# Forgetting, selected-block and dilated attention heads taken two at a time, one in each half of the partitions

## The chip, the cores and the metric

The kernel runs on one core of a Trainium2 chip. The metric is device time in microseconds (us) of one execution; less is better. The median of three runs before the change is 2567.84 us (2560.59 to 2719.17).

## The reference

Two transformer blocks run on one sequence of 256 tokens with 2048 features, all in fp32. The change lies in the first block's mixer: `proj = u @ w_in` is split into the inputs of four kinds of attention, whose outputs are joined and go through `w_out`.

```python
# forgetting ("fox"): 7 heads of 64
s = q @ k * scale + cq[..., None] - cum[:, :, None, :]; p = softmax(causal(s)); o = p @ v
# selected-block ("nsa"): 8 heads of 64 in 2 groups; the keys and values of a group are shared
o = g0 * o_cmp + g1 * o_selected + g2 * o_window        # three softmaxes with three sets of keys
# dilated: 9 heads of 64 in 3 groups of 3; heads i, 3+i, 6+i share a softmax over their log-sums
w = softmax(stack(lses)); o = concat(o_g * w_g)
# differential: 4 heads with two score maps of 64 each and a value of 128
o = (softmax(s0) - lam * softmax(s1)) @ v
h = h + g1 * (concat(o_fox, o_nsa, o_dil, o_diff) @ w_out)
```

The rest (norms, the modulation vectors `c_act @ ada_w`, the gated feed-forward layer, and the second block with a band attention, a recurrent mix and a memory attention) is the same before and after. With 256 tokens, 4 blocks of 64 and 16 blocks to select, every causal block is selected, so each head's scores are plain causal scores.

## The kernel before

Features lie on the partitions. A weight matrix is read in pieces of 512 KB by the SP queue (`piece`, L291), cast by ACT into a rounded part `Wh` (L293), and the rest `Wl` is left by DVE (L294); there are three buffers of each. TensorE then runs eight matmuls of 512 columns with `Wh` (both parts of the activations side by side) and eight of 256 columns with `Wl`, all recorded at L189 as `pd<-s,Wh` and `pd<-s,Wl` (`unit_b`). `unit_a` has the activations stationary instead (`pd<-Wh,s`, `pd<-Wl,s`). Call these the dense stream.

Side work is written as Python generators. After each piece `step` advances every active one to its next `yield`, and `later(n, ...)` starts one n pieces on (`AT`: fox heads 4 pieces apart, nsa heads 5, dilated triples 4). `trickle` adds pieces of the modulation vectors: a 512 KB load (L196) and a weighted sum on DVE (L432), 0.5 to 1.0 of them a piece. A scheduler then fixes each engine's order; every engine follows its own, and waits on semaphores.

A head's side work is: `table` (L196) loads its 128x256 mask and slope table into one of three buffers; `scores` makes the scores of both query blocks in one bank of PSUM with two matmuls (64 rows contracted, 128x256 and 128x128), and a fox head adds two that contract 7 rows for its decay; DVE adds the table and takes the maximum (L590), ACT exponentiates with a sum (L594), and weighs (`weigh`, L600); `pt` transposes the map in three matmuls (L193, `ps<-con,e`) and ACT copies it out (L609); `pv` multiplies by the values (`ps<-pt,s`, 64 output partitions); `put` writes the half-height result as a rounded part (ACT, L627) and a rest (DVE, L628). An nsa head does scores, weighing and transposes twice, and sums three value products (the first, of the compressed branch, shows as `ps<-s 128*64`) in one bank. PSUM has four banks for side work and four for the dense stream.

fp32 matmuls show as two records each, so a 64-row score set (two matmuls) is four records, a fox set eight.

Heads h and h+1 of fox lie in opposite halves of the partitions, as do nsa heads j and j+4. The 24 results of 64 rows fill twelve tiles in the order of the heads.

Of the kernel before, what the change touches and what calls it, by code (L numbers as in the profile page):

```python
# [129 lines left out]
NARROW = {"start"}  # L130

# [16 lines left out]
class Build:  # L148
# [424 lines left out]
    def scores(self, q, k, tab, fox=None):  # L573


        nc = self.nc
        p = self.ps()
        last = fox is None
        self.mm(p[:, 0:256], q[:, 128:256], k, True, last)
        if not last:  # L580
            self.mm(p[:, 0:256], fox[0], fox[1], False, True)
        self.mm(p[:, 256:384], q[:, 0:128], k[:, 0:128], True, last)
        if not last:
            self.mm(p[:, 256:384], fox[0], fox[1][:, 0:128], False, True)
        e = self.tmp((128, 384), tag="e")
        m = self.tiny(2)
        nm = self.tiny(2)
        sm = self.tiny(2)
        for a, (lo, hi, t0) in enumerate(((0, 256, 0), (256, 384, 128))):
            nc.vector.tensor_tensor_reduce(e[:, lo:hi], p[:, lo:hi], tab[:, t0:256], scale=1.0, scalar=-3e38,  # L590
                                           op0=OP.add, op1=OP.max, accum_out=m[:, a:a + 1])
        nc.vector.tensor_scalar(nm, m, -1.0, None, op0=OP.mult)  # L592
        for a, (lo, hi) in enumerate(((0, 256), (256, 384))):
            nc.scalar.activation(e[:, lo:hi], e[:, lo:hi], AF.Exp, bias=nm[:, a:a + 1],  # L594
                                 accum_out=sm[:, a:a + 1])
        return e, m, sm
# [38 lines left out]
    def fox_head(self, h):  # L635
        q, k = self.hq[h], self.hk[h]
        tab = self.table(0)
        yield from self.wait(lambda: self.ncum is not None)
        e, m, sm = self.scores(q, k, tab, (self.sel7[h], self.ncum))
        self.weigh(e, self.recip(sm))  # L640
        yield
        t = self.pt(e)
        yield
        hf = (h % 2) * 64
        p = self.ps()[hf:hf + 64, :256]
        self.pv(p, self.fv[0][:, 64 * h:64 * h + 64], self.fv[1][:, 64 * h:64 * h + 64], t)
        self.put(h, p)

    def fox_cum(self):
# [28 lines left out]
        yield  # L678
        p = self.ps()
        self.mm(p[:7, 0:128], a[:, 0:7], self.C["trif"])  # L680
        self.mm(p[:7, 128:256], a[:, 0:7], self.ones, True, False)
        self.mm(p[:7, 128:256], a[:, 7:14], self.C["trif"], False, True)
        t = self.slot()
        v.tensor_copy(t[:7, :256], p[:7, :256])
        self.ncum = t[:7, :256]
# [100 lines left out]
    def nsa_head(self, h):  # L786
        nc = self.nc
        g = h // 4
        hf = 64 * g
        q = self.nq[h % 4][hf:hf + 64]  # L790
        n = 7 + h
        tab = self.table(1 + h)
        es = []
        yield
        for br, k in ((1, self.nks), (2, self.nkw)):
            e, m, sm = self.scores(q, k[hf:hf + 64], tab)
            f = self.recip(sm)
            for a in range(2):
                nc.vector.tensor_tensor(f[:, a:a + 1], f[:, a:a + 1], self.gate[:, 1 - a, h, br:br + 1], op=OP.mult)
            self.weigh(e, f)  # L800
            es.append(e)
            yield
        ts = [self.pt(e) for e in es]
        yield from self.wait(lambda: self.pct is not None)
        yield
        of = (n % 2) * 64
        p = self.ps()[of:of + 64, :256]
        self.mm(p, self.vcb[:, h, :], self.pct, True, False)
        for b in range(2):
            c = b * 128 + g * 64  # L810
            self.pv(p, self.nv[0][:, c:c + 64], self.nv[1][:, c:c + 64], ts[b], False, b == 1)
        self.put(n, p)

    def dil_triple(self, i):
        nc, v = self.nc, self.nc.vector
        M = self.tiny(6)
        Z = self.tiny(6)
        es = []
        for g in range(3):
            h = 3 * g + i  # L820
            tab = self.table(9 + h)
            yield
            e, m, sm = self.scores(self.dq[h], self.dk[h], tab)
            v.tensor_copy(M[:, 2 * g:2 * g + 2], m)
            v.tensor_copy(Z[:, 2 * g:2 * g + 2], sm)
            es.append(e)
        mx = self.tiny(2)
        v.tensor_tensor(mx, M[:, 0:2], M[:, 2:4], op=OP.max)
        v.tensor_tensor(mx, mx, M[:, 4:6], op=OP.max)
        M3 = M.rearrange("p (g a) -> p g a", g=3)  # L830
        v.tensor_tensor(M3, M3, mx[:, None, :].to_broadcast([128, 3, 2]), op=OP.subtract)
        nc.scalar.activation(M, M, AF.Exp)
        v.tensor_tensor(Z, Z, M, op=OP.mult)
        z = self.tiny(2)
        v.tensor_tensor(z, Z[:, 0:2], Z[:, 2:4], op=OP.add)
        v.tensor_tensor(z, z, Z[:, 4:6], op=OP.add)
        r = self.recip(z)
        v.tensor_tensor(M3, M3, r[:, None, :].to_broadcast([128, 3, 2]), op=OP.mult)
        for g in range(3):
            self.weigh(es[g], M[:, 2 * g:2 * g + 2])  # L840
        yield
        for g in range(3):
            h = 3 * g + i
            n = 15 + h
            t = self.pt(es[g])
            yield
            of = (n % 2) * 64
            p = self.ps()[of:of + 64, :256]
            vv = self.dv[0 if h < 5 else 1]
            c = 64 * (h if h < 5 else h - 5)  # L850
            self.pv(p, vv[0][:, c:c + 64], vv[1][:, c:c + 64], t)
            self.put(n, p)
# [16 lines left out]
    def diff_head(self, h):  # L869
# [4 lines left out]
        for m in range(2):  # L874
            e, _, sm = self.scores(self.fq[h][64 * m:64 * m + 64], self.fk[h][64 * m:64 * m + 64], tab)
            es.append(e)
            fs.append(self.recip(sm))
# [9 lines left out]
        self.pv(p, self.fvv[0][:, 128 * h:128 * h + 128], self.fvv[1][:, 128 * h:128 * h + 128], t)  # L887
# [16 lines left out]
    def mixer(self):  # L904
        self.narrow = "mixer" in NARROW
        I, X = self.I, self.X
        w = "w_in"
        self.consts(1)
        sel = [self.slot(), self.slot()]
        self.load(sel[0][:7, :512], I["const2"][:7, :512])  # L910
        self.load(sel[1][:7, :384], I["const2"][:7, 512:])
# [876 lines left out]
```

## Time and profile before

| what | before |
|---|---|
| runs, median of 3 | 2567.84 us |
| profiled execution, own time | 2565.86 us |
| its span | 2563.7 us |
| PE busy | 2478.7 us (97%) |
| DVE busy | 1793.0 us (70%) |
| ACT busy | 1294.2 us (50%) |
| granted TensorE clock, mean | 0.981 |

The profile is of one execution. Its own time is the span from the first to the last instruction and 2.2 us around it. Busy times are unions of an engine's instructions, so overlapping matmuls count once. In a timeline, rows of like instructions are merged: the first number is the start of the first, the second the time to the end of the last, and `x4` their number. The start of a row to the start of the next row is what the engine spent on it.

### The profile page before, as it was taken

To read this page: it belongs to the slowest core of one execution; us is meant where nothing else is said; L and a number is where in the kernel's file an instruction comes from. 1 tells how busy PE (TensorE), PEld (TensorE's weight loads), DVE (VectorE), ACT (ScalarE), POOL (GpSimd) and SP (SyncE) were. 2 spreads that over 40 slices of the span, in tenths; PEclk is the share of its full clock that TensorE was granted. 3 is DMA by queue.
4 is the path that set the end of the run, shared out by engine and by line. 5 is a ranking of instruction groups with operands and counts; after the bars stand their busy time and mean duration, and the time that the engine had idled before them with its cause. 6 is when DMAs were issued, how large, how long until landed. Compare 5 with 4: busy or idle time off the path is not lost.

```text
span 2563.7 us, 39188 instructions
## 1 busy us (share of the span) xinstructions
PE 2478.7 (97%) x14820; PEld 2124.7 (83%) x14820; DVE 1793.0 (70%) x3371; ACT 1294.2 (50%) x2177; POOL 55.7 (2%) x102
## 2 busy tenths in 40 slices
PE   6889999998799999999999999999999999999999
PEld 5678888777688888888888878888888888888888
DVE  8987777689767765555566887659885666666664
ACT  5354455665544444444455554546553554444443
POOL 0000000000000000000000002000110000000000
PEclk8999999999899999999999999999999999999999
DMA  9998777678578866666655656324554366666675
GB/s 326 340 341 286 247 240 267 203 232 270 181 247 277 277 212 190 192 189 188 188 183 183 204 177 181 108 79 149 166 157 124 97 193 189 189 188 190 189 229 166
DMA packets 161500, 527.57 MB, mean 206 GB/s; under 512 B 22912, under 2 KB 33175, under 8 KB 161184
## 3 DMA queue, kind: packets, MB, share of 16 engines
q1 hardware_dynamic: 157296, 516.41, 62.7%
q0 software_dynamic: 4016, 8.66, 1.1%
q8 instruction: 116, 1.90, 0.3%
q14 instruction: 72, 0.59, 0.1%
HBM read 516.60 MB, written 9.45 MB: 205 GB/s over the span
## 4 chain that ended last, share of the span: by engine, by line
PE 71%; issue 12%; DVE 8%; DMA 5%; ACT 2%; POOL 1%; SPq 0%; DVEq 0%; ACTq 0%; POOLq 0%
PE pd L189 64%; PE ps L189 6%; DVE Wl L294 3%; DVE b L432 2%; DMA b<-in_ada_w_dram 2%; DMA W<-in_w_mem_kv_dram 1%; DMA W<-in_w_out_dram 1%; ACT Wh L293 1%; PE ps L193 1%; DMA W<-in_w_in_dram 1%; POOL q L1283 0%; DMA tq<-qd 0%; DVE dt L224 0%; DVE e L590 0%; DVE q L1061 0%
## 5 line engine op out<-in xcount | busy, mean ns | idle before, releaser
L189 PE MATMUL pd<-s,Wh 128*128 128x512 f32 (+1 forms) x5824 | 1450.2, 391 | 37.5 <-ACT Wh L293 19.1
L294 DVE TENSOR_TENSOR Wl<-W,Wh 128x1024 fp32r<-128x1024 f32 x770 | 927.8, 1207 | 546.7 <-ACT Wh L293 519.8
L293 ACT CAST Wh<-W 128x1024 fp32r<-128x1024 f32 x770 | 796.8, 1036 | 957.6 <-PE pd L189 596.7
L189 PEld LDWEIGHTS pd<-s,Wh 128*128 128x128 f32 x5824 | 1032.5, 192 | 225.9 <-ACT Wh L293 24.1
L189 PEld LDWEIGHTS pd<-s,Wl 128*128 128x128 f32 x5584 | 769.4, 192 | 65.8 <-DVE Wl L294 11.2
L189 PE MATMUL pd<-s,Wl 128*128 128x256 f32 x5584 | 795.8, 285 | 6.8 <-DVE Wl L294 6.7
L432 DVE SCALAR_TENSOR_TENSOR b<-b,tq 128x1024 f32<-128x1024 f32 x192 | 233.0, 1221 | 51.0 <-DMA b<-in_ada_w_dram 50.7
L189 PE MATMUL pd<-Wh,s 128*128 128x512 f32 (+4 forms) x576 | 164.0, 363 | 4.3 <-ACT Wh L293 4.3
L189 PEld LDWEIGHTS pd<-Wh,s 128*128 128x128 f32 x576 | 103.8, 189 | 21.7 <-ACT Wh L293 6.2
L224 DVE TENSOR_TENSOR dt<-pd,dt 128x256 f32<-128x256 f32 x289 | 110.7, 418 | 11.0 <-ACT dt L223 10.3
L189 PE MATMUL pd<-Wl,s 128*128 128x512 f32 (+4 forms) x288 | 105.2, 365 | 5.5 <-DVE Wl L294 5.5
L223 ACT COPY dt<-pd 128x256 f32<-128x256 f32 x289 | 94.6, 370 | 22.8 <-PE pd L189 20.9
L189 PE MATMUL ps<-s 128*128 128x256 f32 (+7 forms) x356 | 88.7, 384 | 4.4 <-DVE tab L1555 2.3
L189 PEld LDWEIGHTS ps<-s 64*128 64x128 f32 (+4 forms) x356 | 57.4, 192 | 27.8 <-issue 13.7
L189 PEld LDWEIGHTS pd<-Wl,s 128*128 128x128 f32 x288 | 54.7, 190 | 16.1 <-DVE Wl L294 8.9
L594 ACT ACTIVATE e<-e,y 128x256 f32<-128x256 f32 x80 | 35.7, 449 | 30.3 <-DVE y L592 30.3
L189 PE MATMUL ps<-q,con 128*128 128x256 f32 x132 | 40.0, 410 | 8.4 <-ACT q L1033 2.9
L209 DVE TENSOR_TENSOR s<-q,s 128x256 fp32r<-128x256 f32 x104 | 40.0, 421 | 5.0 <-ACT s L208 4.7
L208 ACT CAST s<-q 128x256 fp32r<-128x256 f32 x104 | 37.9, 405 | 8.2 <-DVE q L1084 4.9
L189 PE MATMUL ps<-pt,s 128*64 128x128 f32 (+3 forms) x176 | 37.6, 343 | 1.7 <-ACT pt L609 1.7
L600 ACT ACTIVATE e<-e,y 128x256 f32<-128x256 f32 x88 | 35.0, 450 | 6.5 <-DVE y L632 3.8
L590 DVE CUSTOM_DVE_ANT_0 e<-ps,tab 128x256 f32<-128x256 f32 x80 | 26.1, 352 | 16.4 <-PE ps L189 16.1
(291 smaller groups left out, 1400.0 us busy)
## 6 DMA issues: line engine op xcount, KB each, us to landing
W<-in_w_in_dram SPq DMA_DIRECT2D x334, 512.0 KB, 3.7
b<-in_ada_w_dram SPq DMA_DIRECT2D x192, 512.0 KB, 5.4
W<-in_ffn_w_gate_dram SPq DMA_DIRECT2D x88, 512.0 KB, 3.8
W<-in_ffn_w_up_dram SPq DMA_DIRECT2D x88, 512.0 KB, 4.1
W<-in_ffn_w_down_dram SPq DMA_DIRECT2D x80, 512.0 KB, 3.6
W<-in_w_mem_kv_dram SPq DMA_DIRECT2D x32, 512.0 KB, 6.4
W<-in_w_out_dram SPq DMA_DIRECT2D x32, 512.0 KB, 4.4
W<-in_w_o_dram SPq DMA_DIRECT2D x32, 512.0 KB, 4.2
```

Of the source, the lines that this page charges most:

```text
L189: self.nc.tensor.matmul(out, lhsT, rhs, start=start, stop=stop)
L193: self.nc.tensor.transpose(out, in_, self.ident[p0:p0 + n, p0:p0 + n])
L208: self.nc.scalar.copy(out[:, :256], src)
L209: self.nc.vector.tensor_tensor(out[:, 256:], src, out[:, :256], op=OP.subtract)
L223: self.nc.scalar.copy(t, ps[:, 256:512])
L224: self.nc.vector.tensor_tensor(t, ps[:, :256], t, op=OP.add)
L293: nc.scalar.copy(Wh[:, :n], W[:, :n])
L294: nc.vector.tensor_tensor(Wl[:, :n], W[:, :n], Wh[:, :n], op=OP.subtract)
L432: nc.vector.scalar_tensor_tensor(W, W, 1.0, self.crow[half], op0=OP.mult, op1=OP.mult, accum_out=acc[:, k:k + 1])
L590: nc.vector.tensor_tensor_reduce(e[:, lo:hi], p[:, lo:hi], tab[:, t0:256], scale=1.0, scalar=-3e38, op0=OP.add, op1=OP.max, accum_out=m[:, ...
L594: nc.scalar.activation(e[:, lo:hi], e[:, lo:hi], AF.Exp, bias=nm[:, a:a + 1], accum_out=sm[:, a:a + 1])
L600: self.nc.scalar.activation(e[:, lo:hi], e[:, lo:hi], AF.Copy, scale=f[:, a:a + 1])
```

## The change

The three kinds of heads become generators over pairs: fox (0,1), (2,3), (4,5) and 6 alone; nsa (j, j+4); dilated (0,3), (1,4), (6,7) as one generator with two softmax groups, (2,5) and 8 as another. `scores` takes a list of heads and issues the matmuls of all of them in turn, each head in its own bank, and then the softmax of each. `pv` issues the value matmuls in turn, and the two heads of a pair write the two halves of one bank, so that one copy and one subtraction of 128 partitions evacuate both. The fox decay rows are built twice, at partitions 0 and 64, and its selector is loaded twice. Tiles hold other heads than before, so `w_out`'s rows are laid out in the order `HEADS`. The table of fox is loaded once a pair. `AT` gives pairs twice the distance of heads, `q` has 12 buffers instead of 14 and `pt` 4 instead of 3. The differential heads call the same `scores`.

```diff
-BUFS = {"q": 14, "dt": 6, "e": 8, "pt": 3, "tab": 3, "b2": 3, "tq": 1}
+BUFS = {"q": 12, "dt": 6, "e": 8, "pt": 4, "tab": 3, "b2": 3, "tq": 1}
-AT = {"fox": 4, "nsa": 5, "dil": 4, "diff": 4, "pre": 4, "solve": 20, "a": 5, "c": 2}
+AT = {"fox": 8, "nsa": 10, "dil": 8, "diff": 4, "pre": 4, "solve": 20, "a": 5, "c": 2}
+HEADS = (0, 1, 2, 3, 4, 5, 7, 11, 8, 12, 9, 13, 10, 14, 15, 18, 16, 19, 17, 20, 21, 22, 6, 23)
...
-    def scores(self, q, k, tab, fox=None):
...
+    def scores(self, heads):
+        nc, v = self.nc, self.nc.vector
+        ps = [self.ps() for _ in heads]
+        for lo, hi, q0 in ((0, 256, 128), (256, 384, 0)):
+            n = hi - lo
+            for p, (q, k, _, fox) in zip(ps, heads):
+                self.mm(p[:, lo:hi], q[:, q0:q0 + 128], k[:, 0:n], True, fox is None)
+            for p, (_, _, _, fox) in zip(ps, heads):
+                if fox is not None:
+                    self.mm(p[:, lo:hi], fox[0], fox[1][:, 0:n], False, True)
+        out = []
+        for p, (_, _, tab, _) in zip(ps, heads):
...
+            for a, (lo, hi, t0) in enumerate(((0, 256, 0), (256, 384, 128))):
+                v.tensor_tensor_reduce(e[:, lo:hi], p[:, lo:hi], tab[:, t0:256], scale=1.0, scalar=-3e38,
+                                       op0=OP.add, op1=OP.max, accum_out=m[:, a:a + 1])
...
-    def pv(self, o, v0, v1, t, start=True, stop=True):
-        self.mm(o, v0, t[:, 0:256], start, False)
-        self.mm(o[:, 128:256], v1, t[:, 256:384], False, stop)
+    def pv(self, heads, start=True, stop=True):
+        for o, v0, v1, t in heads:
+            self.mm(o, v0, t[:, 0:256], start, False)
+        for o, v0, v1, t in heads:
+            self.mm(o[:, 128:256], v1, t[:, 256:384], False, stop)
+
+    def halves(self, p, heads):
+        return [p[64 * a:64 * a + 64, :256] for a in range(len(heads))]
...
-    def put(self, n, ps):
-        t, h = n // 2, (n % 2) * 64
+    def put(self, t, ps, rows=slice(0, 128)):
         if self.O[t] is None:
             self.O[t] = self.slot(dt=F32R)
-        o = self.O[t][h:h + 64]
-        self.nc.scalar.copy(o[:, :256], ps)
-        self.nc.vector.tensor_tensor(o[:, 256:], ps, o[:, :256], op=OP.subtract)
+        o = self.O[t][rows]
+        self.nc.scalar.copy(o[:, :256], ps[rows, :256])
+        self.nc.vector.tensor_tensor(o[:, 256:], ps[rows, :256], o[:, :256], op=OP.subtract)
...
+    def nsa_heads(self, j):
+        hs = (j, j + 4)
+        rows = (slice(0, 64), slice(64, 128))
+        tabs = [self.table(1 + h) for h in hs]
+        es = []
+        yield
+        for br, k in ((1, self.nks), (2, self.nkw)):
+            maps = self.scores([(self.nq[j][s], k[s], tab, None) for s, tab in zip(rows, tabs)])
+            for h, (e, m, sm) in zip(hs, maps):
...
+                self.weigh(e, f)
+            es.append([e for e, _, _ in maps])
+            yield
+        ts = [[self.pt(e) for e in pair] for pair in es]
...
+        p = self.ps()
+        os = self.halves(p, hs)
+        for o, h in zip(os, hs):
+            self.mm(o, self.vcb[:, h, :], self.pct, True, False)
+        for b in range(2):
...
+            self.pv([(os[g], vv(0, g), vv(1, g), ts[b][g]) for g in range(2)], False, b == 1)
+        self.put(3 + j, p)
```

How TensorE's order moves around an nsa pair, in the middle of the nsa heads (`ps<-s` are scores, `ps<-con,e` transposes, `pd` the dense stream). Before, one head:

```order
L189 MATMUL ps<-s 128x256
L189 MATMUL ps<-s 128x128
L189 MATMUL pd<-s,Wh 128x512 x8
L189 MATMUL pd<-s,Wl 128x256 x8
L189 MATMUL ps<-s 128x256
L189 MATMUL ps<-s 128x128
L189 MATMUL pd<-s,Wh 128x512 x8
L189 MATMUL pd<-s,Wl 128x256 x8
L193 MATMUL ps<-con,e 128x128 x3
```

The third pair now:

```order
L194 MATMUL ps<-s 128x256 x2
L194 MATMUL ps<-s 128x128 x2
L194 MATMUL pd<-s,Wh 128x512 x8
L194 MATMUL pd<-s,Wl 128x256 x8
L194 MATMUL ps<-s 128x256 x2
L194 MATMUL ps<-s 128x128 x2
L194 MATMUL pd<-s,Wh 128x512 x8
L194 MATMUL pd<-s,Wl 128x256 x8
L194 MATMUL pd<-s,Wh 128x512 x4
L198 MATMUL ps<-con,e 128x128 x3
L194 MATMUL pd<-s,Wh 128x512 x2
L198 MATMUL ps<-con,e 128x128 x3
```

The matmuls of two heads stand side by side, and the first transposes come four dense matmuls later than those of the single head did, the second head's another two later.

TensorE's order around the value matmuls of the first fox heads (`ps<-pt,s`). Before, the first head:

```order
L193 MATMUL ps<-con,e 128x128 x3
L189 MATMUL pd<-s,Wl 128x256 x4
L189 MATMUL pd<-s,Wh 128x512 x2
L189 MATMUL ps<-pt,s 64x256
L189 MATMUL ps<-pt,s 64x128
```

The first pair now:

```order
L198 MATMUL ps<-con,e 128x128 x3
L194 MATMUL pd<-s,Wl 128x256 x3
L198 MATMUL ps<-con,e 128x128 x3
L194 MATMUL ps<-pt,s 64x256
L194 MATMUL pd<-s,Wl 128x256
L194 MATMUL pd<-s,Wh 128x512 x2
L194 MATMUL ps<-pt,s 64x256
L194 MATMUL ps<-pt,s 64x128 x2
```

The first value matmul of head 0 stands apart from that of head 1, with three dense matmuls between; the second fox pair has the same, and the third has its last one apart.

The SP queue's order where dilated and nsa heads meet (`tab` are the tables, `W` the pieces of `w_in`, `b` those of the modulation). Before, the tables stand one by one:

```order
L196 DMA tab<-in_tabs_dram 128x256
L291 DMA W<-in_w_in_dram 128x1024
L196 DMA tab<-in_tabs_dram 128x256
L196 DMA b_4756<-in_ada_w_dram 128x1024
L196 DMA tab<-in_tabs_dram 128x256
L291 DMA W<-in_w_in_dram 128x1024 x3
```

Now:

```order
L296 DMA W<-in_w_in_dram 128x1024
L201 DMA tab<-in_tabs_dram 128x256 x5
L296 DMA W<-in_w_in_dram 128x1024
L201 DMA tab<-in_tabs_dram 128x256
L296 DMA W<-in_w_in_dram 128x1024 x3
```

Five table loads stand in a row ahead of a piece of weights, with three table buffers as before.

## Rows read from the trace of the kernel before

**Rows 1.** The page, part 1: busy us, share, instructions, all engines.

```profile
PE 2478.7 (97%) x14820; PEld 2124.7 (83%) x14820; DVE 1793.0 (70%) x3371; ACT 1294.2 (50%) x2177; POOL 55.7 (2%) x102
```

**Rows 2.** Windows: length, busy PE, PEld, DVE, ACT, POOL; clock, DMA share, GB/s.

```profile
255.00:540.00 285.00, 281.90 (x1612) 227.91 (x1611) 207.01 (x578) 154.96 (x368) 1.34 (x3) 0.99 0.72 239
540.00:680.00 140.00, 113.27 (x556) 91.76 (x555) 126.11 (x273) 83.73 (x165) 0.00 (x0) 0.88 0.69 226
```

**Rows 3.** Waits of PE, 255 to 540: waiter, releaser, us, times, longest.

```profile
PE ps L193 <- ACT e L600: 1.8, 2, 1.0
```

**Rows 4.** Timeline of PE: one nsa score set alone.

```profile
403.80 0.28 PE L189 MATMUL pd<-Wl,s 128*128 128x256 f32 x1
403.92 0.28 PE L189 MATMUL pd<-Wh,s 128*128 128x256 f32 x1
404.13 0.92 PE L189 MATMUL ps<-s 64*128 64x256 f32 x4
404.98 0.39 PE L189 MATMUL pd<-Wh,s 128*128 128x256 f32 x1
```

**Rows 5.** Timeline of PE: two score sets in opposite halves.

```profile
481.83 0.93 PE L189 MATMUL ps<-s 64*128 64x256 f32 x8
482.69 0.43 PE L189 MATMUL ps<-pt,s 128*64 128x256 f32 x1
```

**Rows 6.** Timeline of PE: value products of two heads, opposite halves, two banks.

```profile
461.92 0.43 PE L189 MATMUL ps<-pt,s 128*64 128x256 f32 x1
461.93 0.43 PE L189 MATMUL ps<-s 128*64 128x256 f32 x1
```

**Rows 7.** Timelines of PE: one half of a bank alone; halves in turn.

```profile
307.75 2.05 PE L189 MATMUL ps<-s,W 128*64 128x30 f32 x32
309.73 2.11 PE L189 MATMUL pd<-s,Wh 128*128 128x512 f32 x8
...
1661.34 0.64 PE L189 MATMUL ps<-s,e 128*64 128x64 f32 x16
1661.91 0.27 PE L189 MATMUL ps<-con,s 64*64 64x64 f32 x1
```

**Rows 8.** Timeline of PE: one fox score set with its decay rows.

```profile
302.13 2.15 PE L189 MATMUL ps<-s 64*128 64x256 f32 x8
304.21 0.51 PE L189 MATMUL pd<-s,Wh 128*128 128x512 f32 x1
```

**Rows 9.** Timeline of PE: the three value products of an nsa head.

```profile
415.46 0.65 PE L189 MATMUL ps<-s 128*64 128x256 f32 x2
...
417.34 0.96 PE L189 MATMUL pd<-s,Wh 128*128 128x512 f32 x3
```

**Rows 10.** Timeline of PE: the value product of one fox head.

```profile
341.87 0.86 PE L189 MATMUL ps<-pt,s 128*64 128x256 f32 x4
342.67 0.50 PE L189 MATMUL pd<-s,Wl 128*128 128x256 f32 x2
```

**Rows 11.** Lines, 255 to 540: count, busy us, mean ns, idle before and releaser.

```profile
L594 ACT ACTIVATE e<-e,y 128x256 f32<-128x256 f32 x68 | 30.4, 448 | 27.3 <-DVE y L592 27.3
L600 ACT ACTIVATE e<-e,y 128x256 f32<-128x256 f32 x66 | 25.8, 449 | 5.9 <-DVE y L632 3.2 <-DVE y L799 2.7
L594 ACT ACTIVATION_READ_ACCUMULATOR e<-e,y 128x1 f32 x68 | 12.8, 188 | 0.0
L627 ACT CAST s<-ps 64x256 fp32r<-64x256 f32 x24 | 8.8, 365 | 16.5 <-PE ps L189 16.4
L590 DVE CUSTOM_DVE_ANT_0 e<-ps,tab 128x256 f32<-128x256 f32 x68 | 22.1, 353 | 14.0 <-PE ps L189 13.7
L628 DVE TENSOR_TENSOR s<-ps,s 64x256 fp32r<-64x256 f32 x24 | 10.1, 420 | 10.7 <-ACT s L627 10.5
```

**Rows 12.** DMA issues, 255 to 540: count, KB each, us to landing.

```profile
tab<-in_tabs_dram SPq DMA_DIRECT2D x24, 128.0 KB, 3.0
```

**Rows 13.** Windows: the stretch at the lower clock inside the stage.

```profile
326.00:333.00 7.00, 7.00 (x20) 4.91 (x19) 5.98 (x16) 1.54 (x3) 0.00 (x0) 0.51 0.67 226
```

More of the change, by code (lines that the diff above doesn't have):

```diff
@@ L809, in nsa_head, with dil_triples @@
         for b in range(2):
[L810 to L814, printed above, removed]
+            vv = lambda t, g: self.nv[t][:, b * 128 + g * 64:b * 128 + g * 64 + 64]
+            self.pv([(os[g], vv(0, g), vv(1, g), ts[b][g]) for g in range(2)], False, b == 1)
+        self.put(3 + j, p)
+    def dil_triples(self, run, pairs):
         nc, v = self.nc, self.nc.vector
[L816 to L821, printed above, removed]
-            yield
[L823 to L840, printed above, removed]
@@ new lines, in dil_triples @@
+        M = {i: self.tiny(6) for i in run}
+        Z = {i: self.tiny(6) for i in run}
+        es = {}
+        for hs, _ in pairs:
+            tabs = [self.table(9 + h) for h in hs]
+            yield
+            maps = self.scores([(self.dq[h], self.dk[h], tab, None) for h, tab in zip(hs, tabs)])
+            for h, (e, m, sm) in zip(hs, maps):
+                g, i = divmod(h, 3)
+                v.tensor_copy(M[i][:, 2 * g:2 * g + 2], m)
+                v.tensor_copy(Z[i][:, 2 * g:2 * g + 2], sm)
+                es[h] = e
@@ L841, in dil_triple @@
+        for hs, _ in pairs:
+            for h in hs:
+                g, i = divmod(h, 3)
+                self.weigh(es[h], M[i][:, 2 * g:2 * g + 2])
         yield
[L842 to L845, printed above, removed]
+        for hs, tile in pairs:
+            ts = [self.pt(es[h]) for h in hs]
             yield
[L847 to L852, printed above, removed]
+            p = self.ps()
+            vv = lambda t, h: self.dv[h // 5][t][:, 64 * (h % 5):64 * (h % 5) + 64]
+            if len(hs) == 2:
+                self.pv([(o, vv(0, h), vv(1, h), t) for o, h, t in zip(self.halves(p, hs), hs, ts)])
+                self.put(tile, p)
+            else:
+                self.pv([(p[64:128, :256], vv(0, hs[0]), vv(1, hs[0]), ts[0])])
+                self.put(tile, p, slice(64, 128))
@@ L873, in diff_head @@
         yield
-        for m in range(2):
-            e, _, sm = self.scores(self.fq[h][64 * m:64 * m + 64], self.fk[h][64 * m:64 * m + 64], tab)
+        rows = (slice(0, 64), slice(64, 128))
+        for e, _, sm in self.scores([(self.fq[h][s], self.fk[h][s], tab, None) for s in rows]):
             es.append(e)
@@ L955, in mixer @@
         self.begin(self.fox_cum)
-        for h in range(7):
-            self.later(AT["fox"] * h, lambda h=h: self.fox_head(h))
+        for i, hs in enumerate(((0, 1), (2, 3), (4, 5), (6,))):
+            self.later(AT["fox"] * i, lambda hs=hs: self.fox_heads(hs))
         self.rate = RATES[1]
@@ L971, in mixer @@
         self.begin(self.nsa_compress)
-        for h in range(8):
-            self.later(8 + AT["nsa"] * h, lambda h=h: self.nsa_head(h))
+        for j in range(4):
+            self.later(8 + AT["nsa"] * j, lambda j=j: self.nsa_heads(j))
         self.rate = RATES[2]
@@ L1573, in a_head @@
         c = slice(128 * (h % 4), 128 * (h % 4) + 128)
[L1574 removed]
+        self.pv([(p, self.av[h // 4][0][:, c], self.av[h // 4][1][:, c], t)])
         nc.vector.tensor_copy(q, p)
```

119 lines of the change are left out of this document (59 added, 60 removed).

## The prediction

> **What bounds the kernel now.** I read the page first. PE is busy 97% of the span, DVE 70%, ACT 50% [rows 1]. That is an average, so the windows by stage come next. The heads that change work between 255 us, where the fox sums begin, and 540 us, where the differential heads on `w_out` take over. In those 285 us PE is busy 281.9, DVE 207.0 and ACT 155.0, the clock is at 0.99 and the DMA engines at 0.72 [rows 2]. From 540 to 680 the picture turns: PE 113 of 140, DVE 126 [rows 2]. So in the first stage whatever PE no longer does shortens the run, until something else is late; in the second it would not. The waits agree: in the first stage PE stood for the transposes' input only twice, 1.8 us in all [rows 3]. What PE spends on one head I take from its timeline, from the start of a row to the start of the next.
>
> **What side by side costs.** One nsa score set takes PE from 404.13 to 404.98, 0.85 us, and is entered 0.21 us after the start of the last dense matmul, where like dense matmuls follow each other after 0.12 [rows 4]: 0.94 us alone, 0.85 in a longer run. At 481.83 two sets of opposite halves stood next to each other by chance, and eight records took 0.86 us [rows 5]. So the second set was free: matmuls that contract different halves run at the same time. For outputs in different halves, two value products started at 461.92 and 461.93 [rows 6], in two banks. In one bank, as the change has it, I find only a smaller form: the compression writes 30 columns into one half with 32 records in 1.98 us, 62 ns each, and the second block's recurrence 64 columns into the two halves in turn with 16 in 0.57, 36 ns each [rows 7].
>
> **The sum**, against the profiled execution's own 2565.86 us (2.0 below the median of the runs).
>
> - Scores of nsa and dilated heads: 16 + 9 sets. One pair was already together, so 24 passes; now 8 + 4 pairs and one single, 13. 11 fewer at 0.9, between 0.85 and 0.94: -9.9.
> - Fox scores: 2.08 us a set [rows 8] and 0.09 for entry, 7 passes to 4: 3 x 2.17 = -6.5. That pairs of the 7-row matmuls overlap no row shows. If they did not, about half of 2.08 would come back for each of three pairs, 3.1; if they do, nothing. I take nothing, since it is the nearest case, halves of the contracted rows, that is seen free [rows 5].
> - Value products of nsa: 1.88 us a head [rows 9] and 0.09; 8 passes to 4: 4 x 1.97 = -7.9.
> - Value products of dilated heads: 0.80 [rows 10] and 0.09, 9 passes to 5; about half of one was free already [rows 6]: -3.1.
> - Value products of fox: 7 passes to 4 would be 2.7, but the order sets the heads of all three pairs partly apart, with dense matmuls between. I take a third: -0.9.
> - Decay rows twice: three more small matmuls, six records; by the small ones of the compression, 62 ns each [rows 7]: +0.4.
>
> Together -27.9 us of PE.
>
> At nothing I cost these. Evacuation: 24 half-height pairs of 365 ns on ACT and 420 on DVE [rows 11] become 13; 4.0 and 4.6 us fall away on engines that PE hardly waits for. The two more selector loads of 14 and 10 KB stand in the SP queue before the mixer's first pieces, where the weights are ahead. Three table loads fewer. The five tables in a row on the SP queue: each waits for a table in use to be read, and a piece of weights stands behind them; a load lands in 3.0 us [rows 12]. What covers it is that three pieces stand ahead in their ring; uncovered it is one landing, or two where one table waits for the other, 3 to 6 us, once. The smaller `q` ring: the order of every engine is unchanged after `w_out`, so I see nothing late. The differential heads were side by side already.
>
> **New waits.** A pair's second map comes out later. DVE reduces four pieces instead of two, 0.35 us each [rows 11], and on ACT two more exponentials (448 and 188 ns each) and two more weighings (25.8 us over 66, 0.39 each) stand in front of its transposes [rows 11]: 2.05 us. The order puts the first head's transposes four dense matmuls later than before, about 1 us, and the second's two more. From below a gain of 1.8 us is possible, if the two old waits go [rows 3]; from above, all of it is seen in each of 13 groups, 26.7. I take 4 us, near the lower row, because DVE stands idle 78 of the 285 us and ACT 130 [rows 2], and DVE's busy share rises only to about 0.79 (202 of 257).
>
> The Trainium skill, "TensorEngine Tiling (Array Packing)", section "PSUM Bottleneck", speaks against the change here: tiling makes TensorE faster, but not the copies out of PSUM, which may become the bottleneck. By that rule the gain would shrink to what the first rival gives; the rows above show neither engine near its limit in this stage.
>
> 2565.9 - 27.9 + 4 = **2542 us**, 0.9% less. The stretch of 7 us at clock 0.51 [rows 13], half of which is lost, stood on the tiny matmuls of the compression and a fox head; whether it comes again is open, 3.5 us either way.
>
> **Rivals.**
>
> 1. *The softmax chain takes the place of PE.* In each of 13 groups PE stands at the transposes. If only the two further reductions show, 0.7 x 13 = 9 us, the run ends at 2547 to 2551; with all of ACT's 2.05 us, at 2565. For it: bursts double, and DVE already did the modulation sums between them. Against: [rows 3]. 2551 to 2565, chance 0.23.
> 2. *The halves do not run together in one bank, nor the 7-row matmuls.* Then only the first term and about half of the second stay, 13 us: with the waits 2557. For it: no row shows 256 columns in one bank. Against: [rows 7]. 0.06.
> 3. *Slower.* The place is the same, but both heads' transposes wait, because ACT takes the two maps in turn: 4.1 us in each of 13 groups is 53, less 27.9: 2591. It decides from 27.9/13 = 2.1 us a group on. Against: the distance in the order grew. 0.06; over 2% slower (2619) would take 6.2 us a group, so 0.02 of that.
> 4. *More than forecast*: the dense stream also loses its entries and the lower clock, under 2530: 0.05.
>
> The forecast, 2530 to 2551, has 0.60.
>
> **Range and chances.** 2526 to 2566: below it only a part of the fourth case, above it the third and the noise of runs (2560.59 to 2567.84 is 0.3%). About 2% is what a measurement of this kernel can tell from no change. A gain of 2% would need 51 us, nearly twice what PE gives up, so faster 0.03; slower 0.03; the same 0.94.
>
> **What would show it.** In the trace after: a paired nsa score set of eight records in about 0.86 us; a fox pair of sixteen in about 2.1; the twenty records of an nsa pair's values in about 1.9; the sum of PE's waits for L600's weighing in this stage under 7 us; `w_out`'s differential heads beginning some 24 us earlier, and from there the same time to the end. Wrong would be: value rows of a pair one after the other; PE idle ahead of transposes in most groups; a gain in this stage that the stage bound by DVE takes back.

## The result, and the profile after the change

The changed kernel took 2531.57 us, median of 4 runs (2525.20 to 2538.22); its ratio to the kernel before is 0.9877, with a 95% interval from 0.9834 to 0.9920. (One run of before, of 2719.17 us, was in a slow state of the chip and is not in that ratio.) Measured again beside the first experiments it took 2533.68 us, 0.9878 (0.9859 to 0.9897), by that ratio some 31 us less than before. The forecast was 2542 us, between 2526 and 2566: right in sign and range, and 8 to 10 us short in size.

The page of the changed kernel, part 1, answers to [rows 1]:

```profile
PE 2454.7 (97%) x14826; PEld 2111.1 (83%) x14826; DVE 1788.3 (71%) x3361; ACT 1289.6 (51%) x2166; POOL 55.6 (2%) x102
```

TensorE has 24.0 us less of busy time and six more matmul records. To see where in the run, the traces are laid over each other at the dense matmuls, of which both have 12272. Their order is the same but for 36 of them, all between the 2281st and the 2466th, where matmuls with `Wh` and with `Wl` stand in other turns: the 1187th is the start of the stage of the heads, the 2279th its end. Those two marks stand at 255.2 and 540.4 us before and at 253.7 and 519.5 after. Windows of the changed kernel between these marks, and from there to the 2770th (680.1 before), columns as in [rows 2]:

```profile
253.70:519.50 265.80, 258.10 (x1620) 215.49 (x1619) 206.46 (x575) 152.31 (x360) 1.05 (x3) 0.97 0.76 261
519.50:650.50 131.00, 106.81 (x553) 86.62 (x552) 122.86 (x268) 82.56 (x164) 0.00 (x0) 0.92 0.68 232
```

Against [rows 2] the first stage is 19 us shorter: TensorE is busy 23.8 us less and stands 4.6 us more (3.1 before, 7.7 now). The second is shorter too, 131.0 us for 139.7, where the forecast had no change. After it the two traces run side by side: 1866.5 us from there to the 12201st dense matmul before, 1867.2 after.

What two heads cost side by side, TensorE's timeline: a fox pair, an nsa pair of scores, and the value products of an nsa pair. Each block ends with the next dense matmul, whose start ends the count.

```profile
275.02 2.17 PE L194 MATMUL ps<-s 64*128 64x256 f32 x16
277.13 0.74 PE L194 MATMUL pd<-s,Wh 128*128 128x512 f32 x2
...
395.07 0.65 PE L194 MATMUL ps<-s 128*64 128x256 f32 x4
395.55 1.55 PE L194 MATMUL ps<-pt,s 128*64 128x256 f32 x16
397.03 0.39 PE L194 MATMUL pd<-Wl,s 128*128 128x256 f32 x1
...
412.31 0.92 PE L194 MATMUL ps<-s 64*128 64x256 f32 x8
413.16 0.73 PE L194 MATMUL pd<-s,Wh 128*128 128x512 f32 x2
```

Sixteen fox records take 2.11 us where eight took 2.08 [rows 8], eight nsa records 0.85 where four took 0.85 [rows 4], twenty value records 1.96 where ten took 1.88 [rows 9]: the second head is free in all three. Of the other nsa pairs' values one took 1.88 us and one 2.54, in which the second head's records stop for 0.4 us in the middle; one runs on into other heads' values. Added up from the start of each record to the next, the scores of the stage went from 38.1 to 23.0 us and the value products from 27.4 to 17.3.

TensorE's waits in this stage, as [rows 3]:

```profile
PE ps L198 <- ACT e L610: 4.5, 2, 2.7
PE ps L194 <- DVE y L696: 1.5, 1, 1.5
```

The transposes' wait for the weighing rose from 1.8 to 4.5 us, in two stops. This is the longer one, on TensorE's timeline:

```profile
419.90 1.09 PE L194 MATMUL pd<-s,Wh 128*128 128x512 f32 x4
423.71 0.90 PE L198 MATMUL ps<-con,e 128*128 128x128 f32 x3 [2.72 <-ACT e L610]
```

The window of the 3.4 us behind it:

```profile
423.60:427.00 3.40, 3.29 (x12) 2.80 (x13) 2.95 (x10) 2.60 (x10) 0.00 (x0) 0.50 0.89 304
```

TensorE stands 2.72 us, and then works at 0.50 of its clock, the lower of the two levels, for 3.4 us. What the weighing waits for stands on DVE's timeline: the reductions of the second head's map begin only after a modulation sum, and a subtraction for `Wl` stands ahead of the products with the gates (L822) that the weighing needs.

```profile
418.80 1.22 DVE L437 SCALAR_TENSOR_TENSOR b<-b,tq 128x1024 f32<-128x1024 f32 x1
419.95 0.08 DVE L437 DVE_READ_ACCUMULATOR b<-b,tq 128x1 f32 x1
419.95 0.42 DVE L599 CUSTOM_DVE_ANT_0 e<-ps,tab 128x256 f32<-128x256 f32 x1
...
421.31 1.20 DVE L299 TENSOR_TENSOR Wl<-W,Wh 128x1024 fp32r<-128x1024 f32 x1
422.43 0.22 DVE L822 TENSOR_TENSOR y<-y,gates 128x1 f32<-128x1 f32 x2
```

On ACT a cast of weights stands just ahead of the weighing:

```profile
421.92 1.03 ACT L298 CAST Wh<-W 128x1024 fp32r<-128x1024 f32 x1
422.86 1.49 ACT L610 ACTIVATE e<-e,y 128x256 f32<-128x256 f32 x4
```

The evacuations, from the lines of the stage, which answer to L627 and L628 in [rows 11]: eleven of full height at the same price as half-height ones.

```profile
L643 DVE TENSOR_TENSOR s<-ps,s 128x256 fp32r<-128x256 f32 x11 | 4.5, 421 | 1.4 <-ACT s L642 1.3
L642 ACT CAST s<-ps 128x256 fp32r<-128x256 f32 x11 | 4.1, 372 | 6.5 <-PE ps L194 6.5
```

### The profile page after: what moved, and what is told of

Same layout as the page of the kernel before. It is cut to its first block, busy times and chain, and to the rows that moved or that the text cites. A ratio compares the mean times of both kernels' runs of the same rounds, so it can differ in the third digit from the quotient of the medians.

```text
span 2534.3 us, 39180 instructions
## 1 busy us (share of the span) xinstructions
PE 2454.7 (97%) x14826; PEld 2111.1 (83%) x14826; DVE 1788.3 (71%) x3361; ACT 1289.6 (51%) x2166; POOL 55.6 (2%) x102
## 4 chain that ended last, share of the span: by engine, by line
PE 79%; DVE 11%; DMA 6%; issue 2%; ACT 2%; SPq 0%; DVEq 0%; ACTq 0%
PE pd L194 69%; PE ps L194 9%; DVE Wl L299 3%; DMA b<-in_ada_w_dram 2%; DVE b L437 2%; DMA W<-in_w_in_dram 2%; PE ps L198 1%; ACT Wh L298 1%; DMA W<-in_w_mem_kv_dram 1%; DMA W<-in_w_out_dram 1%; DVE dt L229 0%; DVE q L208 0%; DVE q L207 0%; DVE s L214 0%; DMA s<-in_b_w_dram 0%
## 5 line engine op out<-in xcount | busy, mean ns | idle before, releaser
L229 DVE TENSOR_TENSOR dt<-pd,dt 128x256 f32<-128x256 f32 x289 | 110.7, 418 | 12.1 <-ACT dt L228 11.6
L194 PE MATMUL ps<-s 64*128 64x256 f32 (+7 forms) x356 | 69.0, 375 | 4.8 <-DVE s L1578 3.0
L194 PEld LDWEIGHTS ps<-s 64*128 64x128 f32 (+4 forms) x356 | 45.7, 186 | 22.9 <-issue 8.5
L194 PEld LDWEIGHTS ps<-q,con 128*128 128x128 f32 x132 | 23.1, 197 | 16.8 <-ACT q L525 4.5
L1110 ACT ACTIVATE q<-dt 128x256 f32<-128x256 f32 x44 | 18.2, 415 | 30.3 <-DVE dt L229 30.3
```

The costliest lines, as they stand in the source:

```text
L194: self.nc.tensor.matmul(out, lhsT, rhs, start=start, stop=stop)
L229: self.nc.vector.tensor_tensor(t, ps[:, :256], t, op=OP.add)
L1110: nc.scalar.activation(gs[b], self.total(ps), AF.Silu)
```

## The experiments

The theory: the gain is TensorE's passes, saved because matmuls of opposite halves run at the same time. Its first rival, "bunching": it comes from fewer changes between dense and side work and from fewer evacuations, whatever the halves.

**Both kernels once more.** No edit.

> The changed kernel once more, as the yardstick of the others and for a second trace of it. Side by side (the change saves TensorE's passes, 26 us of side work, in the stage of the fox, nsa and dilated heads): 2526 to 2538 us, and score and value records of that stage within 1 us of the first trace (scores 23.0, values 17.3 us). Clock (about 9 of the 29 us lie in the short stretch of the first differential heads, 21.2 us before and 12.4 after, and are no part of the change but the lower clock that happened to fall there before): that stretch again under 14 us if the change removed the cause, up to 21 if it was chance.

Measured: 2533.68 us, 0.9878 (0.9859 to 0.9897). Added up from the start of each record to the next, scores and value products of the first stage take 23.0 and 17.9 us, within 0.7 of the first trace. The stretch of the first differential heads took 12.4 us again. This second run of the change is called the control below. The experiments were run in three sets, each with its own runs of before, whose medians were 2566.54 (the set of the control), 2563.86 and 2566.19 us; across sets a difference of 2 or 3 us between medians says nothing, and the ratios are the better measure. The kernel before again:

> The kernel before once more, for a second trace of it. In the first trace the stage behind the heads (540 to 680 us) took 139.7 us with the clock at half speed for 34.1 of them; in the traces of the change 131.0 and 133.0, with 20.5 and 23.9. Theory, a disturbed trace (the change does nothing there, the first trace of before had more of the lower clock than others): 133 to 136 us now. Rival, the change helps there too (its heads end sooner and DVE comes into the stage with less to do): 138 to 141 again.

Measured: 2564.73 us, 0.9988 (0.9974 to 1.0002). Windows of the two stages in the control:

```profile
254.10:517.00 262.90, 258.02 (x1621) 214.66 (x1620) 206.02 (x574) 152.36 (x360) 0.92 (x2) 0.97 0.78 264
517.00:650.00 133.00, 107.71 (x554) 86.32 (x553) 123.01 (x268) 82.37 (x165) 0.00 (x0) 0.91 0.68 228
```

And of the kernel before again:

```profile
258.20:545.50 287.30, 284.08 (x1614) 229.08 (x1613) 206.72 (x576) 155.26 (x367) 0.00 (x0) 0.98 0.71 236
545.50:682.20 136.70, 108.84 (x556) 88.09 (x555) 125.41 (x271) 83.56 (x166) 0.00 (x0) 0.91 0.70 231
```

Over two traces each, the first stage went from 286.3 to 264.4 us and the second from 138.2 to 132.0. So 136.7 lies between the two answers that were written down: at the same clock, 0.91, the second stage is 3.7 us shorter with the change, and the other 2.5 of the 6.2 lie in the first traces, where before had more of the low clock (0.88 in [rows 2], 0.92 with the change). The first stage also starts 2.8 us earlier on average with the change; in all the traces of these kernels its start lies anywhere from 251.5 to 258.2 us, so this is no sign of a gain ahead of it.

**Pairs in the same half.** The score matmuls of fox and nsa pairs contract the same 64 rows; TensorE's order is the same, row for row.

```diff
-enumerate(((0, 1), (2, 3), (4, 5), (6,)))          # fox
+enumerate(((0, 2), (1, 3), (4, 6), (5,)))
-        hs = (j, j + 4)                             # nsa
-        rows = (slice(0, 64), slice(64, 128))
+        hs = (2 * j, 2 * j + 1)
+        g = j // 2
+        rows = (slice(64 * g, 64 * g + 64),) * 2
```

> Fox pairs (0,2), (1,3), (4,6) and 5 alone, nsa pairs (0,1), (2,3), (4,5), (6,7): the score matmuls of a pair contract the same half of the partitions. TensorE's order, the softmax, the value products, the evacuation and the dilated pairs stay as in the change. Side by side: a fox pair of 16 records takes 4.2 us in place of 2.1 and an nsa pair of 8 records 1.7 in place of 0.85, 3 x 2.08 + 8 x 0.85 = 13.0 us more, so about 2545. Rival, bunching (the gain comes from half as many changes between dense and side work and half as many evacuations): within 2 us of the change.

Measured: 2537.28 us, 0.9889 (0.9875 to 0.9904). A fox pair and an nsa pair on its TensorE timeline:

```profile
276.98 3.46 PE L194 MATMUL ps<-s 64*128 64x256 f32 x16
280.37 0.74 PE L194 MATMUL pd<-s,Wh 128*128 128x512 f32 x2
...
416.47 1.57 PE L194 MATMUL ps<-s 64*128 64x256 f32 x8
417.97 0.50 PE L194 MATMUL pd<-s,Wh 128*128 128x512 f32 x1
```

3.39 us in place of 2.11, and 1.50 in place of 0.85. So the halves do run together, and bunching alone falls. By the time of the runs this could not be said: 0.9889 and the control's 0.9878 have intervals that overlap; it is the records that show it. And the size was wrong: I had written 4.2 and 1.7. A single nsa set of 0.85 us is 0.65 of work and 0.20 that an unbroken group of such matmuls costs once, however many sets stand in it. In the same way a fox set, which changes between 64 and 7 rows three times and then goes back to the dense stream, is 1.28 of work and four times 0.20: 2.08 alone [rows 8], 2 x 1.28 + 0.80 = 3.36 for two in one half. So bunching has a part as well: scores took 38.1 us before, 30.5 in this run and 23.0 in the control. Of the 15.1 us, 7.5 are the opposite halves of the fox and nsa pairs; by 0.65 us for each of the four dilated pairs, which stayed in opposite halves here, the halves have about 10 in all, and the other 5 (both are estimates) are prices paid once for two heads. Had I looked for two sets next to each other in the same half, TensorE's timeline of before had them:

```profile
485.18 1.57 PE L189 MATMUL ps<-s 64*128 64x256 f32 x8
486.68 0.43 PE L189 MATMUL ps<-pt,s 128*64 128x256 f32 x1
```

And of 7.5 us more of score records only 3.6 show in the time. TensorE stands 3.5 us in this stage here, 4.9 in the control: its wait for the weighing falls from 1.8 to 0.7 us. It also spends 10.2 us at half clock here and 13.7 in the control, worth half of the difference, 1.7 us. That the softmax gains time from what TensorE does more is likely, but not shown apart from the clock.

**Head after head.** Matmuls of a pair in the order A, A, B, B.

```diff
-        for lo, hi, q0 in ((0, 256, 128), (256, 384, 0)):
...
-            for p, (q, k, _, fox) in zip(ps, heads):
+        for p, (q, k, _, fox) in zip(ps, heads):
+            for lo, hi, q0 in ((0, 256, 128), (256, 384, 0)):
...
         for o, v0, v1, t in heads:
             self.mm(o, v0, t[:, 0:256], start, False)
-        for o, v0, v1, t in heads:
             self.mm(o[:, 128:256], v1, t[:, 256:384], False, stop)
```

> Scores and value products of a pair are issued head after head (A, A, B, B) and not in turn; both still stand next to each other and in opposite halves. Halves go on their own (as in the trace of before at 481.83, where eight records of two heads in this order took 0.86 us): an nsa or dilated pair still 0.86, a fox pair 2.1, and the time within 3 us of the change. Rival, in order (a matmul runs beside the one issued next to it alone): of each pair only the last of A and the first of B meet, a pair takes about 1.5 in place of 0.86 and a fox pair 3.7, and values likewise: 12 x 0.6 + 3 x 1.6 + 10 = 22 us more.

Measured: 2545.06 us, 0.9922 (0.9905 to 0.9940). A fox pair and an nsa pair on its TensorE timeline:

```profile
278.49 4.23 PE L194 MATMUL ps<-s 64*128 64x256 f32 x16
282.65 0.73 PE L194 MATMUL pd<-s,Wh 128*128 128x512 f32 x2
...
416.65 0.93 PE L194 MATMUL ps<-s 64*128 64x256 f32 x8
417.51 0.50 PE L194 MATMUL pd<-s,Wh 128*128 128x512 f32 x1
```

Both theories were half right. For nsa and dilated scores the turn does nothing: 0.86 us; the value products of an nsa pair took 1.93. In the nsa score pair A's and B's first matmuls start 0.014 us apart, though A's second stands between them in the order. Two of the three fox pairs take 4.16, twice a single set: with a change between 64 and 7 rows between A's matmuls, B's do not pass A's. In the first pair the scheduler put B's first 64-row matmul directly behind A's; it takes 3.13, where the change takes 2.49. So alternating is worth 2.05 us in two fox pairs and 0.64 in the first, and nothing in the other pairs' scores. All scores together take 4.7 us more than in the control, which is these three; the time is 11.4 us longer. The scheduler also laid the work around them in another order. In the traces the first stage is 5.1 us longer and the second 1.7; where the rest of the other 6.7 us comes from stays open.

**Value products in the same half.** Both heads' products go to the lower 64 partitions of two banks, evacuated apart.

```diff
     def halves(self, p, heads):
-        return [p[64 * a:64 * a + 64, :256] for a in range(len(heads))]
+        return [(p, self.ps())[a][0:64, :256] for a in range(len(heads))]
...
-        self.put(3 + j, p)
+        self.put2(3 + j, os)      # a copy and a subtraction for each half
...
```

> The value products of a pair write the same (lower) 64 partitions of two banks, each evacuated at half height; scores as in the change. Side by side: twenty records of an nsa pair take 3.8 us in place of 1.96, those of a dilated or fox pair 1.6 in place of 0.8: 4 x 1.84 + 7 x 0.8 = 13.0 us; the traces give only 10.2 between before and the change, so 10 to 13 more, 2542 to 2545. Rival, bunching: within 2 us of the change. The further evacuations, 4.0 us on ACT and 4.6 on DVE, should cost nothing under either.

Measured: 2549.84 us, 0.9938 (0.9920 to 0.9955). The twenty records of an nsa pair on its TensorE timeline:

```profile
400.42 1.08 PE L194 MATMUL ps<-s 128*64 128x256 f32 x4
401.33 2.76 PE L194 MATMUL ps<-pt,s 128*64 128x256 f32 x16
404.03 0.50 PE L194 MATMUL pd<-Wh,s 128*128 128x256 f32 x2
```

3.61 us in place of 1.96. All value records take 26.7 us, 8.8 more than in the control, and the time is 16.2 us longer, more than I gave it; the first stage is 275.2 us, 12.3 more. Here nothing is given back: the wait for the weighing is 4.1 us in this trace and 1.8 in the control. The halves account for the 8.8 us. The rest is not theirs alone: the scheduler laid the side work out anew (257 of 527 side matmul records stand behind the same dense matmul as in the control), the first stage has 17.1 us at half clock for 13.7, and the second is 3.2 us longer. For the values bunching gives little: 27.4 us before, 26.7 here. The theory stands for values too.

**Two banks.** As above, but the products stay in opposite halves.

```diff
+        return [(p, self.ps())[a][64 * a:64 * a + 64, :256] for a in range(len(heads))]
...
```

> The two value products of a pair go to two banks, in opposite halves, and each half is evacuated by itself; scores and the turns of the matmuls as in the change. Side by side: the value records take what they took (twenty of an nsa pair about 1.96 us), ACT and DVE have 11 more half-height evacuations, 4.0 and 4.6 us, beside TensorE's work: within 3 us of the change (2531 to 2536). Rival, evacuation counts: the 8.6 us show at least in half, 2538 or more.

Measured: 2534.84 us, 0.9895 (0.9880 to 0.9910), within 1.2 us of the control. The twenty records of an nsa pair took 2.00 us, and all value records 17.8 (17.9 in the control). Its evacuations, from the lines of the first stage:

```profile
L638 DVE TENSOR_TENSOR s<-ps,s 64x256 fp32r<-64x256 f32 x22 | 9.2, 420 | 4.1 <-ACT s L637 3.6
L637 ACT CAST s<-ps 64x256 fp32r<-64x256 f32 x22 | 8.1, 367 | 10.7 <-PE ps L194 10.2
```

4.0 us on ACT and 4.7 on DVE come back and cost nothing that can be measured: the first stage is 265.7 us, in the two traces of the change 265.8 and 262.9. But by the ratios, 0.9895 and 0.9878, the run is 4.4 us slower than the control, and half of the 8.6 us, which the rival asks for, is 4.3; the intervals overlap. So one bank and one evacuation a pair are not shown to be a part of the gain, and a few microseconds are not excluded. The run above, with the same evacuations but the products in the same half, took 15.0 us more (11 by the ratios), so the evacuations were not what it lost by.

**Before, with the differential heads' transposes later.** The largest single piece of the second stage's gain lies in its first 61 dense matmuls. The window of that stretch in the first trace of before:

```profile
540.40:561.50 21.10, 18.44 (x90) 14.21 (x89) 17.60 (x43) 16.87 (x31) 0.00 (x0) 0.84 0.77 245
```

In the second:

```profile
545.50:563.40 17.90, 15.77 (x92) 12.09 (x90) 17.66 (x43) 14.66 (x29) 0.00 (x0) 1.00 0.77 244
```

And in the first trace of the change:

```profile
519.50:531.90 12.40, 12.40 (x74) 10.41 (x73) 12.37 (x36) 10.53 (x23) 0.00 (x0) 1.00 0.75 253
```

This compares unlike work: the third head's scores stand ahead of the end of the stretch before and behind it with the change. At the 2350th dense matmul, where both have had them, the two traces of before stand at 23.3 and 20.0 us and both of the change at 17.0, so at the same clock 3.0 us are left of the gain and not 5.5. Before, the second differential head's transposes stand behind the 2328th dense matmul and wait for DVE; with the change they stand behind the 2339th and do not (the third head's then wait 1.52 us, for 0.72 before). So the kernel before got a step more there:

```diff
             v.scalar_tensor_tensor(es[0][:, lo:hi], es[1][:, lo:hi], ...)
         yield
+        yield
         t = self.pt(es[0])
```

> The kernel before with the transposes of the differential heads one piece of weights later; nothing in pairs. Theory of the wait (in the kernel before, the second differential head's softmax came late behind a modulation sum on DVE, TensorE stood 1.5 + 0.6 + 0.6 us, the clock then fell for 6.8 us; the change's other order of DVE took that away, 8.8 us of its gain): that stretch, 21.2 us, falls under 15, and the two later heads, which stood too, gain 2 to 4 each, so 8 to 14 us less than before: 2552 to 2559. Rival, the clock fell there by chance: 2560 to 2567 as before.

Measured: 2563.70 us, 1.0003 (0.9993 to 1.0012). Its windows, of both stages and of the stretch:

```profile
253.10:539.80 286.70, 284.96 (x1623) 230.15 (x1622) 207.85 (x577) 156.01 (x370) 1.22 (x3) 0.98 0.71 238
539.80:674.50 134.70, 106.16 (x546) 87.50 (x545) 125.25 (x270) 79.80 (x161) 0.00 (x0) 0.90 0.71 233
539.80:555.80 16.00, 14.31 (x82) 11.70 (x81) 15.60 (x41) 10.84 (x24) 0.00 (x0) 1.00 0.73 239
```

The stretch fell to 16.0 us and the stage by 2.0 against the second trace of before, yet the runs are the same to 0.1%. In TensorE's order the step shows as earlier scores (the third head's behind the 2328th dense matmul and not the 2339th), not as later transposes: the second head's stand behind the 2327th. The theory of the wait falls as a source of gain: TensorE's wait for the differential heads' weighing falls from 2.9 to 0.9 us, but that for `Wh` rises from 2.2 to 6.0, in a stage where DVE is busy 93%.

**The change with later transposes.**

```diff
             es.append([e for e, _, _ in maps])
             yield
+        yield
         ts = [[self.pt(e) for e in pair] for pair in es]
```

(and the same in the fox pairs)

> The change with the transposes of fox and nsa pairs one piece of weights later. In the change TensorE stood twice for a pair's weighing, 2.7 and 1.8 us, each time followed by 3.4 us at half clock. Waits of the softmax eat a part of the gain: both stops and the clock behind them go, 4.5 + 2 x 1.7 = 8 us, so about 2526. Rival, something else becomes late (the exponentials' eight buffers, the four banks): no gain, 2531 to 2538, with other waits in place of L610's.

Measured: 2532.55 us, 0.9881 (0.9867 to 0.9896), no gain. The windows of both stages:

```profile
253.90:511.20 257.30, 250.91 (x1616) 210.19 (x1615) 204.71 (x572) 151.68 (x359) 1.22 (x3) 0.99 0.79 270
511.20:646.00 134.80, 109.52 (x558) 87.87 (x557) 124.44 (x272) 82.00 (x166) 0.00 (x0) 0.91 0.69 225
```

The first stage is 5.6 us shorter than in the control, with the clock at 0.99; the second takes 1.8 of that back, and the rest cannot be seen in the runs. What went is the low clock, 3.4 us of it in the first stage for 13.7 in the control, and not TensorE's stops: the wait for the weighing is 1.3 us, but all stops together are 6.4 for 4.9. So the 8 us that I had put on stops and clock were too many, and of the 5.6 that came, half of those 10.3 us, 5.1, are the clock's.

**Fox scores regrouped, differential heads later.** For the second query block the decay rows come first. The differential heads have the further `yield` of two runs above.

```diff
...
+            if lo == 0:                # 64 rows, then 7
+                main(True, False); decay(False, True)
+            else:                      # 7 rows, then 64
+                decay(True, False); main(False, True)
```

> The change with two edits: the differential heads' transposes one piece later as in the run above, and in fox scores the decay rows of the second query block ahead of its 64-row matmuls, so that the array goes from 64 rows to 7 and back twice a pair and not three times. Theory of a price per switch (0.2 us: sets of the same half cost 1.50 for two and 0.85 for one, so 0.65 for work and 0.20 for the switch): a fox pair 1.9 us in place of 2.1, together 0.8 us; differential heads 3 and 4 stand no more, 2 to 4 us each: 2525 to 2529. Rival, that stage is bound by DVE, which is 98% busy there, and only moves the wait: 2531 to 2535.

Measured: 2535.36 us, 0.9884 (0.9867 to 0.9901). The fox pair on its TensorE timeline:

```profile
277.23 1.98 PE L194 MATMUL ps<-s 64*128 64x256 f32 x16
279.13 0.73 PE L194 MATMUL pd<-s,Wh 128*128 128x512 f32 x2
```

1.90 us, as the price per switch has it: 1.28 + 3 x 0.20 = 1.88. Both orders add onto the same columns of PSUM equally often, so the price goes with the change of rows and not with the adding. In the time neither edit shows, and the second stage takes 133.0 us as in the control, as the rival has it.

**More of the modulation's sums in the first stage.** The second stage looks bound by DVE and the first by TensorE, with DVE at 0.78; so sums were moved forward. The second and third of these runs also have the later transposes of fox and nsa pairs and the regrouped fox scores.

```diff
-RATES = (0.5, 0.8, 0.8, 0.8, 1.0)
+RATES = (0.5, 0.9, 0.9, 0.9, 1.0)     # 1.0, 1.0, 1.0 in the last of the three
```

> The change with 0.9 in place of 0.8 modulation sums a piece while the heads of the mixer are worked on, so that seven of the sums (1.22 us of DVE and 512 KB each) are done before 520 us in place of after. The stage behind is 93% busy on DVE. If DVE sets that stage and TensorE the one before: about 7 x 1.3 = 9 us less, 2524. Rival, the sums stand in front of the heads' softmax on DVE and TensorE waits for it: 2533 to 2540, with more of L610's wait in the first stage.

> The same, with the transposes of fox and nsa pairs one piece later and the fox scores' decay rows regrouped (1.9 us a pair in place of 2.1), so that the softmax has the time that the sums take. If both stages are as told: 9 us from the sums, 4 from the waits, 0.8 from the regrouping: 2520. Rival, what one stage gives the next takes back, since DVE is behind all along: 2530 to 2535.

> As the run before with 1.0 sums a piece, fourteen of them moved to before 520 us. If DVE's share in the first stage (0.79, with this about 0.86) still leaves the softmax in time: 2512 to 2516. Rival, waits in the first stage grow: no better than the run before.

Measured: 2535.96 us, 0.9878 (0.9855 to 0.9901); 2530.13, 0.9854 (0.9833 to 0.9875); 2541.39, 0.9891 (0.9865 to 0.9918). The window of the second stage in the first of them:

```profile
515.70:647.80 132.10, 109.04 (x554) 89.46 (x553) 118.77 (x258) 81.56 (x164) 0.00 (x0) 0.90 0.63 210
```

And in the second:

```profile
514.30:644.90 130.60, 106.70 (x554) 86.87 (x553) 118.68 (x258) 81.60 (x164) 0.00 (x0) 0.92 0.64 212
```

DVE has 4.2 us less to do there than in the control, the stage is 0.9 and 2.4 us shorter. That is a weaker test than was planned: the first stage has six more sums than in the control (64 for 58), but the second only three fewer (27 for 30), since later sums move up as well. So DVE's busy share is high, but that it sets the stage by itself is not borne out. In the first of them TensorE's waits there and in the stage before for `Wl` rise from 5.2 to 11.5 us and for `Wh` from 1.6 to 7.5. The second run, sums and later transposes together, has the lowest median of all; its interval overlaps that of the change, so it is not shown to be better. In the third the rival holds. Its first stage:

```profile
256.70:526.30 269.60, 257.97 (x1630) 217.17 (x1629) 218.02 (x599) 151.24 (x360) 0.00 (x0) 0.96 0.80 279
```

It is 6.7 us longer than in the control: TensorE stands 11.6 us there, 6.4 of them in one wait for DVE, and 20.5 us of the stage are at half clock.

## Why the prediction was right, and where it was short

- **What bounds the stage**: right. TensorE's busy time fell by 23.8 us in the first trace and the stage by 19 (by 21.9 on average over two traces each).
- **The sum, -27.9 us**: right in size. Scores gave up 15.1 us and values 10.2, where the terms were 16.4 and 11.9 with the entries of 0.09 us, which do not lie in these records. The whole can be read off the busy time too: in the first traces the stage has 13.7 us at half clock with the change and 6.8 before; half of the difference, 3.4, added to 23.8 gives 27.2, an estimate. Each kind of pair came as forecast: 0.85 us for 0.86, 2.11 for 2.1, 1.96 for 1.9. What was wrong is what the price is made of: I took a single set's 0.85 us as work, and 0.20 of it is paid once per group. For the sum this made no difference, since a pair saves both.
- **That 7-row pairs overlap**, which no row showed: they do, issued in turn (2.11 us), and do not head after head (4.16).
- **Evacuation at nothing**: borne out within the noise by the two banks. The Trainium skill, "TensorEngine Tiling (Array Packing)", section "PSUM Bottleneck", has copies out of PSUM as what may bind after a fourfold speedup of TensorE by tiling. Here, with two heads side by side, eleven copies more on each engine moved the median by 1.2 us and the ratio by 0.17%, both within the intervals.
- **New waits, +4 us**: right. TensorE stands 4.6 us more in the first trace and 1.8 in the second. The runs with fox and nsa scores in the same half and with later transposes moved these waits about, but turned none into time that the runs show.
- **"From there the same time to the end"**: this step failed, and most of the 8 to 10 us by which the forecast was short lie here. The stage of the differential heads is 6.2 us shorter on average over two traces each. 2.5 of it go with the clock. Of the other 3.7 the rows show two things: DVE has 2.4 us less to do (125.4 to 123.0), because it comes into the stage one piece of weights and one sum ahead, and the wait for the differential heads' weighing is 0.7 shorter (2.9 to 2.2):

```profile
PE ps L193 <- DVE e L881: 2.9, 3, 1.5
PE ps L198 <- DVE e L911: 2.2, 2, 1.5
```

The order is not the same there either: the 36 dense matmuls that changed their turns stand in this stage, and 3.0 of the 3.7 us are there by the 2350th. That one of these brings the time was only argued: the runs that moved sums brought less than they took from DVE. It stays open.

- **The median of before**: the forecast started from a profiled execution of 2565.86 us; the runs of before had medians of 2563.86 to 2566.54 in the later comparisons, so this made no more than 2 us.

**The rivals**: that the halves do not run together in one bank is refuted by the 1.96 us; the softmax chain did take TensorE's place, as the first rival has it, but in two groups of thirteen (4.5 us); the slower case did not come.

## What to carry to other kernels

Price a small matmul group by two terms, its work and what the array takes to enter and leave its shape, and read both off the trace by finding one group alone and two next to each other. Groups that contract or write opposite halves share the first term and, side by side, the second too; where shapes alternate within a group, issue like shapes of both together. Expect a part of what TensorE gives up to come back as waits, and see in the next stage whether it stays: here, in most of the experiments, a few microseconds of a stage did not show in the runs.

## What the runs showed of the hardware that I had not expected

- A change of shape in the array has a price of about 0.20 us, the same from 64 rows to 7, back, and to the dense stream. It is worked out from 0.85, 1.50 and 2.08 us; 3.39, 2.11, 1.90 and 4.16 us then come out to 0.04 us. For value products, 64 columns wide, the same subtraction gives about 0.15 (2 x 1.88 for two heads apart, 3.61 for two in the same half).
- Matmuls of the second head pass those of the first where the order has them behind (A, A, B, B in 0.86 us, the first two of each 0.014 us apart), but not where such a change stands between (4.16 us).
- ACT and DVE copy and subtract from partitions 0 to 63 to partitions 64 to 127 at the price of doing it within a half: in the run with values in the same half, where eleven of 22 cross, 0.363 to 0.374 us a copy and 0.407 to 0.420 a subtraction; with two banks, where none does, 0.367 and 0.420 on average.
